# Stepping an encoder's background work twice per unit of weights

## The chip, the cores and the metric

One Trainium2 chip, one core. The metric is device microseconds of one execution, taken as the median of several; lower is better. The engines that matter here: TensorE (PE, matrix products), VectorE (DVE) and ScalarE (ACT) for elementwise work, GpSimd (POOL), and SyncE (SP), which issues the transfers. All of them work through their own queues in order, and meet at semaphores.

## The reference

Two layers of an encoder on 256 tokens of width 2048, all in float32. With `c` a condition vector, each layer computes

```
mod  = silu(c) @ ada_w + ada_b                # six vectors of 2048: scale, shift, gate, twice
h0   = rmsnorm(x) * (1 + scale0) + shift0
qA kA vA qB kB vB gateA gateB = split(h0 @ w_in)   # 8 heads of 128 in A (2 groups of k, v), 8 in B
a    = softmax(rotary, normed qA kA^T, |i-j| <= 128, sink per head) vA
b    = softmax(normed qB kB^T + 2-D relative bias, neighbourhood) vB
x   += gate0 * ((sigmoid(gateA) * (a @ w_proj_a) + sigmoid(gateB) * (b @ w_proj_b)) @ w_out)
h1   = rmsnorm(x) * (1 + scale1) + shift1
u    = depthwise conv over the tokens (width 3) of (h1 @ w_up);  g, v = halves of u, 5632 wide each
x   += gate1 * ((silu(g) * v) @ w_down)
```

## The kernel before, in words

**The stream.** All the weights of a layer lie in memory in the order in which they are used, cut into 232 units of 16 blocks of 128 x 128 floats (1 MB). `unit_steps` loads a unit (`w`, L337) and splits it into two float32r parts, in two halves of 8 blocks each: ScalarE casts the high part (`hl`, L348), VectorE subtracts it from the weights for the low part (L349). In the listings `hl_54_0` is the first half of unit 54. TensorE multiplies with both parts. `tokens` (L464 to 466) is used for q, k and v, three products 512 columns wide for each four blocks and each 128 tokens; `features` calls `feature_block` for everything else, either three products 256 wide per block (L395 to 397; the third takes the low part of the weights) or one of 512 and one of 256 (L391, L392). `Stream.at` counts the blocks of the current unit, `UB` is 16.

**The modulation.** The `mod` vectors are worked out on VectorE, 128 x 2048 products (`aw`, L248) in a fixed number by each unit (`plan`). They lie on the VectorE queue among the `hl` subtracts.

**The background.** The heads of the mixers, and the chunks of the normed `h`, are Python generators that emit a few instructions at each step. An object `bg` of the class `Paced` keeps the running ones with a rate and an accumulator. Whenever `features` or `tokens` have used up a unit (`at == UB`), they call `tick`: it first runs what was deferred to this point, then adds the rate to each accumulator and takes one step for each whole number in it. So the rate is steps per unit. It then lets `plan` emit modulation products.

The jobs are these. `attention` (L981 on) is one job for all 16 heads of a layer. One step of it gives each live head its next part, and starts one new head if its q and k are ready (`ready`, which for layer 0 has to be 3). The parts of a head, in `attend`: the scores `sc` (L727) and the softmax with them (DVE L730 with the mask and row maximum, `nm` L736; ACT exponentials L739, `es` L742; DVE `den` L743 and `ri` L745; ACT scaling of `p`, L747); then the transposes of `p` with the split of the result (`tp` L758, `pT`, ACT L481 and DVE L484); then the products with v (`po` L766) and their split (`oA`, L769 and L770). So one step holds `po` of head i, `tp` of head i+1, `sc` of head i+2 and the start of head i+3. In layer 1 the transposes are not TensorE's: VectorE transposes blocks of 32 x 32 (L326) and GpSimd copies them to their places (L320, 16 copies). Rates: `ATT` is 1.288 in layer 0 and 0.4 in layer 1; once the A heads are through (`attended`, ahead of the projection `proj_a`, which reads `oA` of all eight A heads, and which begins behind unit 52 in layer 0), layer 0 goes on with 0.36. The normed chunks of the next `h` have the rates `H_RATE`, 2.7 for the first and 1.7 for the second sub-layer. q and k are normed by instructions that `bg.defer` puts at unit ends (`qrs` L535 on GpSimd, `qn` L661 on VectorE, `packB` L698 on ScalarE).

**The order.** A list scheduler orders each engine's queue from the order in which the program emits the instructions and from its own costs. In layer 0 it may move the heads' instructions among those of the stream; in layer 1 they stay in the order of the program. So a step that is emitted half a unit sooner changes the queues of all engines around it.

## Time and profile before

| | |
|---|---|
| median of 3 runs | 2582.82 us (2582.07 to 2588.05) |
| the profiled execution | 2584.3 us |
| its span | 2581.7 us |
| mean granted clock of TensorE | 0.998 |
| TensorE busy | 2547.9 us, 99% |
| VectorE, ScalarE, GpSimd busy | 86%, 56%, 10% |
| waits of TensorE for `hl` of VectorE at L397, in all | 7.1 us in 9 |
| wait of TensorE for `p` at `tp` | 3.6 us in 4 |
| wait of TensorE for `packB` at `sc` | 2.6 us in 1 |

The span is the time between the first and the last instruction of the profiled execution. A row of the timeline gives the start and the length of an instruction (or of several alike in a row, xN), engine, line, operation, what is written and from what, and in brackets how long the engine had been idle before it and which instruction ended that. A row of the waits gives who waited for whom, the total, the number and the longest. Matrix products overlap, so their spacing is shorter than their length.

### The profile page before, as it was taken

The numbers are of one execution on the slowest core, as the hardware profiler recorded it, in microseconds if no ns is written. First come the engines' busy times: TensorE is split into PE (matmuls) and PEld (weight loads), VectorE is DVE, ScalarE is ACT, GpSimd is POOL, SyncE is SP. The second block draws the span as 40 slices with busy tenths as digits, with TensorE's granted clock in tenths as the row PEclk, the third lists the DMA queues.
The fourth block names the chain that finished last, engine by engine and source line by source line (L and its number), as shares of the span: only waits on it lengthen the run. The fifth ranks groups of instructions, "written<-read, shape, count | busy, mean of one in ns | idle before, by whom it ended". The sixth has DMA issues, their size and how long they took to land.

```text
span 2581.7 us, 43544 instructions
## 1 busy us (share of the span) xinstructions
PE 2547.9 (99%) x17324; PEld 2378.3 (92%) x17324; DVE 2212.6 (86%) x3227; ACT 1454.8 (56%) x2432; POOL 263.1 (10%) x345
## 2 busy tenths in 40 slices
PE   8999999999999999999999999999999999999999
PEld 7999899999999999999998879999999999999998
DVE  8998998998998899799987778879889987766775
ACT  5445765456663665466565566654576546644663
POOL 0001100000000000000003668730000000000000
PEclk9999999999999999999999999999999999999999
DMA  9998789986778778777767667778848775555554
GB/s 370 352 349 306 263 299 356 335 315 227 259 292 307 258 285 297 291 279 279 281 226 271 262 229 264 258 284 332 309 175 294 291 295 197 206 201 197 204 202 147
DMA packets 102158, 699.97 MB, mean 271 GB/s; under 512 B 12866, under 2 KB 15170, under 8 KB 18114
## 3 DMA queue, kind: packets, MB, share of 16 engines
q1 hardware_dynamic: 101954, 697.20, 73.0%
q8 instruction: 135, 2.21, 0.3%
q14 instruction: 69, 0.56, 0.1%
HBM read 695.06 MB, written 2.10 MB: 270 GB/s over the span
## 4 chain that ended last, share of the span: by engine, by line
PE 70%; DVE 14%; DMA 6%; ACT 4%; issue 4%; POOL 2%; SPq 0%; ACTq 0%; DVEq 0%; POOLq 0%
PE ps L391 31%; PE ps L392 15%; DVE hl L349 5%; PE ps L397 5%; PE ps L395 5%; PE ps L396 5%; DVE aw L248 4%; DMA aw<-in_aw 3%; PE ps_t L465 2%; PE ps_t L464 2%; PE ps_t L466 2%; ACT hl L348 2%; DMA w<-in_ws 2%; POOL p L320 1%; DVE x L1108 1%
## 5 line engine op out<-in xcount | busy, mean ns | idle before, releaser
L349 DVE TENSOR_TENSOR hl<-w,hl 128x1024 fp32r<-128x1024 f32 x928 | 1130.3, 1224 | 215.4 <-ACT hl L348 213.1
L348 ACT CAST hl<-w 128x1024 fp32r<-128x1024 f32 x928 | 964.7, 1046 | 587.0 <-PE ps L392 253.8
L391 PE MATMUL ps<-h,hl 128*128 128x512 f32 x2432 | 796.8, 382 | 0.0
L392 PE MATMUL ps<-h,hl 128*128 128x256 f32 x2432 | 662.9, 273 | 0.0
L391 PEld LDWEIGHTS ps<-h,hl 128*128 128x128 f32 x2432 | 459.7, 189 | 64.0
L392 PEld LDWEIGHTS ps<-h,hl 128*128 128x128 f32 x2432 | 466.9, 192 | 0.0
L248 DVE CUSTOM_DVE_ANT_0 aw<-aw,cact,ab 128x2048 f32<-128x2048 f32 x189 | 443.8, 2349 | 14.0 <-DMA aw<-in_aw 13.4
L395 PE MATMUL ps<-h,hl 128*128 128x256 f32 x896 | 247.3, 276 | 1.9 <-DVE ri L745 0.8
L397 PE MATMUL ps<-h,hl 128*128 128x256 f32 x896 | 245.9, 276 | 0.6 <-DVE hl L349 0.6
L396 PE MATMUL ps<-h,hl 128*128 128x256 f32 x896 | 246.4, 275 | 0.0
L465 PE MATMUL ps_t<-hl,h 128*128 128x512 f32 x576 | 220.4, 383 | 4.8 <-DVE hl L349 4.5
L464 PE MATMUL ps_t<-hl,h 128*128 128x512 f32 x576 | 217.7, 383 | 3.8 <-ACT h L571 2.4
L466 PE MATMUL ps_t<-hl,h 128*128 128x512 f32 x576 | 219.0, 381 | 0.0
L395 PEld LDWEIGHTS ps<-h,hl 128*128 128x128 f32 x896 | 171.9, 192 | 3.1 <-PE ps L397 0.9
L396 PEld LDWEIGHTS ps<-h,hl 128*128 128x128 f32 x896 | 172.0, 192 | 0.4 <-DVE h L572 0.2
L397 PEld LDWEIGHTS ps<-h,hl 128*128 128x128 f32 x896 | 171.6, 192 | 0.8 <-DVE hl L349 0.8
L391 PE MATMUL ps<-act_o,hl 128*128 128x512 f32 x512 | 170.5, 382 | 0.0
L1135 DVE SCALAR_TENSOR_TENSOR u<-both,cw,u 128x255 f32<-128x255 f32 x304 | 146.0, 480 | 3.8
L397 PE MATMUL ps<-merged,hl 128*128 128x256 f32 x512 | 140.8, 276 | 3.5 <-DVE hl L349 3.5
L395 PE MATMUL ps<-merged,hl 128*128 128x256 f32 x512 | 140.7, 275 | 0.4 <-ACT hl L348 0.4
L396 PE MATMUL ps<-merged,hl 128*128 128x256 f32 x512 | 140.6, 275 | 0.0
L392 PE MATMUL ps<-act_o,hl 128*128 128x256 f32 x512 | 139.6, 273 | 0.0
(242 smaller groups left out, 4867.6 us busy)
## 6 DMA issues: line engine op xcount, KB each, us to landing
w<-in_ws SPq DMA_DIRECT2D x463, 1024.0 KB, 4.9
aw<-in_aw SPq DMA_DIRECT2D x189, 1024.0 KB, 5.0
p<-in_bias SPq DMA_DIRECT2D x16, 256.0 KB, 4.9
x<-in_xT SPq DMA_DIRECT2D x4, 512.0 KB, 5.4
aw_o<-in_aw SPq DMA_DIRECT2D x2, 1024.0 KB, 12.8
out<-x SPq DMA_DIRECT2D x16, 128.0 KB, 2.2
w<-in_ws SPq DMA_DIRECT2D x2, 512.0 KB, 12.1
aw_b<-in_aw SPq DMA_DIRECT2D x1, 1024.0 KB, 17.9
```

The lines of the kernel that those rows point to most:

```text
L248: product = nc.vector.tensor_tensor_reduce(out=raw[:], in0=raw[:], in1=cact[:], scale=1.0, scalar=ab[:, i : i + 1], op0=ALU.mult, op1=ALU. ...
L348: nc.scalar.copy(hl[:, 0], r)
L349: nc.vector.tensor_tensor(out=hl[:, 1], in0=r, in1=hl[:, 0].bitcast(F32), op=ALU.subtract)
L391: nc.tensor.matmul(ps[:], hi, act.both, start=first, stop=False)
L392: nc.tensor.matmul(ps[:, :S], lo, act.high, start=False, stop=last)
L395: nc.tensor.matmul(out, hi, act[0], start=first, stop=False)
L396: nc.tensor.matmul(ps[:, :S], hi, act[1], start=False, stop=False)
L397: nc.tensor.matmul(out, lo, act[0], start=False, stop=last)
L464: nc.tensor.matmul(ps[:], xh, hi, start=kc == kcs[0], stop=False)
L465: nc.tensor.matmul(ps[:], xh, lo, start=False, stop=False)
L466: nc.tensor.matmul(ps[:], xl, hi, start=False, stop=kc == kcs[-1])
L1135: nc.vector.scalar_tensor_tensor(out=u[:, to], in0=ps[:, of], scalar=w[:, j : j + 1], in1=u[:, to], op0=ALU.mult, op1=ALU.add)
```

## The change

The accumulators gain half the rate at a time, and this is done twice per unit: `step` is what was the second half of `tick`, `tick` calls it at the unit's end as before, and a new `Stream.passed` calls it alone when half of the unit's blocks are used. The deferred instructions and the modulation's plan stay at unit ends. Rates are as they were.

```diff
             for fn in later:
                 fn()
+            self.step()
+
+        def step(self):
             for job in list(self.jobs):
-                job[2] += job[1]
+                job[2] += job[1] / 2
                 while job[2] >= 1.0:
...
+        def passed(self):
+            if self.at == UB:
+                self.tick()
+            elif self.at == UB // 2:
+                bg.step()
+
...
                     feature_block(ps, hl, j, act_of, i == 0, i == len(acts) - 1)
-                    if self.at == UB:
-                        self.tick()
+                    self.passed()
...
                     warm(WARM_ROW)
-                if self.at == UB:
-                    self.tick()
+                self.passed()
```

In the listings of the change line numbers are 3 higher from L291 on, and 7 higher behind L475 (`sc` L734, `tp` L765, `po` L773, `es` L749, `hl` L351 and L352).

What that does to the queues is shown at three places. The first is TensorE in layer 0 from the transposes of head 7 on (`tp`, with the scores of the next head, `sc`, put between them). Before:

```order
L758 MATMUL tp<-ident,p 128x128 x3
L727 MATMUL sc<-packB_0_224 128x256
L397 MATMUL ps_53_8_0_3375<-oA_4_2734,hl_52_1_3347 128x256
L395 MATMUL ps_53_8_0_3375<-oA_4_2734,hl_52_1_3347 128x256
L396 MATMUL ps_53_8_0_3375<-oA_4_2734,hl_52_1_3347 128x256
L766 MATMUL po<-pT,vA_1_2826 128x256 x2
L397 MATMUL ps_53_8_0_3375<-oA_4_2734,hl_52_1_3347 128x256
L395 MATMUL ps_53_8_0_3375<-oA_6_2848,hl_52_1_3347 128x256
L396 MATMUL ps_53_8_0_3375<-oA_6_2848,hl_52_1_3347 128x256
L397 MATMUL ps_53_8_0_3375<-oA_6_2848,hl_52_1_3347 128x256
L766 MATMUL po<-pT,vA_1_2826 128x256 x4
L395 MATMUL ps_53_16_0_3416<-oA_0_2446,hl_53_0_3419 128x256
```

With the change:

```order
L765 MATMUL tp<-ident,p 128x128 x3
L734 MATMUL sc<-packB_0_224 128x256
L773 MATMUL po<-pT,vA_1_2880 128x256 x6
L398 MATMUL ps_52_16_0_3303<-oA_7_3000,hl_52_0_3306 128x256
L398 MATMUL ps_53_8_0_3337<-oA_7_3000,hl_52_1_3309 128x256
L398 MATMUL ps_53_16_0_3378<-oA_7_3000,hl_53_0_3381 128x256
L398 MATMUL ps_54_8_0_3412<-oA_7_3000,hl_53_1_3384 128x256
L399 MATMUL ps_52_16_0_3303<-oA_7_3000,hl_52_0_3306 128x256
L400 MATMUL ps_52_16_0_3303<-oA_7_3000,hl_52_0_3306 128x256
L765 MATMUL tp<-ident,p 128x128
L734 MATMUL sc<-packB_0_224 128x256
L765 MATMUL tp<-ident,p 128x128 x3
```

The six products `po` and the first uses of `oA_7` now stand directly behind the transposes of head 7, and those of head 8 follow six products later, where a run of other products stood between them.

The second is VectorE at the same place, up to the low half of unit 54. Before:

```order
L770 TENSOR_TENSOR oA_7_2939<-po,oA_7_2939 128x256
L484 TENSOR_TENSOR vB_0_3209<-packB_0_224,vB_0_3209 128x256
L497 SCALAR_TENSOR_TENSOR ya_222<-ya_222,ps_52_16_0_3341 128x256
L745 RECIPROCAL ri<-den 128x2
L497 SCALAR_TENSOR_TENSOR ya_222<-ya_222,ps_53_8_0_3375 128x256
L497 SCALAR_TENSOR_TENSOR ya_222<-ya_222,ps_53_16_0_3416 128x256
L349 TENSOR_TENSOR hl_54_0_3516<-w_54_3514,hl_54_0_3516 128x1024
```

With the change (rows of the row maxima and repeats left out):

```order
L777 TENSOR_TENSOR oA_7_3000<-po,oA_7_3000 128x256
L491 TENSOR_TENSOR vB_0_3278<-packB_0_224,vB_0_3278 128x256
L248 ISA aw_46_3698,mod_172<-aw_46_3698,cact,ab_173 128x2048
L491 TENSOR_TENSOR pT<-tp,pT 128x512
L737 ISA p,m<-sc,p 128x256
L504 SCALAR_TENSOR_TENSOR ya_222<-ya_222,ps_52_16_0_3303 128x256
L743 TENSOR_SCALAR nm<-m 128x2
L504 SCALAR_TENSOR_TENSOR ya_222<-ya_222,ps_53_8_0_3337 128x256
L504 SCALAR_TENSOR_TENSOR ya_222<-ya_222,ps_53_16_0_3378 128x256
L504 SCALAR_TENSOR_TENSOR ya_222<-ya_222,ps_54_8_0_3412 128x256
L352 TENSOR_TENSOR hl_54_0_3479<-w_54_3477,hl_54_0_3479 128x1024
```

Between `oA_7` and the subtract for unit 54 there are now a modulation product, the `pT` of head 8, and the scores of the head behind it.

The third is ScalarE in layer 1, at the exponentials of head 1 (L739, then L746) and the cast of head 0's transposed weights (`pT`, L481, then L488). Before:

```order
L348 CAST hl_30_0_15157<-w_30_15155 128x1024
L348 CAST hl_30_1_15160<-w_30_15155 128x1024
L481 CAST qA_2_15118<-packA_14134 128x256
L481 CAST pT<-p 128x512
L739 ACTIVATE p,den<-p,nm 128x256 x2
L742 ACTIVATE es<-nm,sink_14275 128x2
L348 CAST hl_31_0_15239<-w_31_15237 128x1024
L348 CAST hl_31_1_15242<-w_31_15237 128x1024
L747 ACTIVATE p<-p,ri 128x256 x2
```

With the change:

```order
L351 CAST hl_30_0_15157<-w_30_15155 128x1024
L488 CAST qA_2_15106<-packA_14134 128x256
L746 ACTIVATE p,den<-p,nm 128x256 x2
L749 ACTIVATE es<-nm,sink_14275 128x2
L351 CAST hl_30_1_15160<-w_30_15155 128x1024
L754 ACTIVATE p<-p,ri 128x256 x2
L488 CAST pT<-p 128x512
L351 CAST hl_31_0_15239<-w_31_15237 128x1024
```

The exponentials and the scaling of head 1 now stand ahead of the cast `pT`, and one weight cast stands between them.

## The prediction

> **What bounds the kernel now.** I read the page's first part, then the waits of TensorE over the whole span, then the stretches in which those waits lie, then the instructions around the two largest.

> ```profile
> span 2581.7 us, 43544 instructions
> PE 2547.9 (99%) x17324; PEld 2378.3 (92%) x17324; DVE 2212.6 (86%) x3227; ACT 1454.8 (56%) x2432; POOL 263.1 (10%) x345
> ```

> TensorE is busy for 2547.9 of 2581.7 us. The change adds and removes no matrix product, so all it can win is in the remaining 34 us, and about half of that is the start. The waits of TensorE (total us, times, longest) say what is left:

> ```profile
> PE ps L397 <- DVE hl L349: 7.1, 9, 1.7
> PE ps_t L465 <- DVE hl L349: 4.5, 5, 2.8
> PE tp L758 <- ACT p L747: 3.6, 4, 2.4
> PE sc L727 <- ACT packB L698: 2.6, 1, 2.6
> PE ps L395 <- DVE ri L745: 0.8, 1, 0.8
> ```

> `tp` and `sc` are the transposes and the scores of the mixers' heads, so 3.6, 2.6 and 0.8 us belong to what the change re-times; of the 4.5 us before `ps_t`, 2.78 lie among the heads of layer 1 (below). The stretches of 50 us (PE, PEld, DVE, ACT and POOL busy, TensorE clock, DMA share, GB/s) show where the heads run:

> ```profile
> 250.00:300.00 50.00, 46.73 (x241) 40.25 (x240) 49.31 (x89) 37.52 (x106) 11.80 (x4) 1.00 0.79 286
> 300.00:350.00 50.00, 48.79 (x385) 45.65 (x385) 48.03 (x107) 40.95 (x107) 2.45 (x1) 1.00 0.66 236
> 350.00:400.00 50.00, 49.90 (x427) 48.82 (x426) 48.04 (x80) 30.02 (x58) 0.00 (x0) 1.00 0.92 340
> 1450.00:1500.00 50.00, 47.70 (x235) 41.26 (x233) 36.05 (x56) 32.89 (x69) 31.98 (x49) 1.00 0.61 232
> 1500.00:1550.00 50.00, 46.43 (x224) 40.69 (x225) 41.65 (x69) 31.89 (x73) 29.02 (x47) 0.93 0.63 232
> 1550.00:1600.00 50.00, 50.00 (x410) 48.82 (x409) 42.75 (x68) 32.76 (x69) 43.82 (x61) 1.00 0.73 262
> ```

> In layer 0 (250 to 350) VectorE is full: 49.31 and 48.03 of 50. TensorE lacks 3.27 and 1.21 us, and one unit of weights needs two `hl` subtracts of VectorE, so there the order of VectorE's work decides. In layer 1 (1450 to 1550) VectorE has 8 to 14 us to spare per stretch, TensorE lacks 2.30 and 3.57, the clock drops to 0.93, and GpSimd is in the chain. Two places then, one of each kind.

> **The change, first place: the eight A heads of layer 0.** Before, the accumulator gains 1.288 at each unit's end and so takes two steps in units 44, 47 and 51. Now it gains 0.644 twice. The start of head 0 needs `ready` to be 3, which comes in unit 44; the half step at unit 44's middle is spent on nothing, and the half steps from then on give one turn less before the stream reaches `proj_a`: head 7's products `po` come at the end of unit 52 instead of 51. By the orders, 24 matmuls of 512 columns more precede the first scores (235 matmuls, nearly all so wide, fill 47.70 us in 1450 to 1500, 0.20 each: 4.9 us). The stretch between the first scores and the first transposes holds the same TensorE work (7.1 us counted in both orders), so the largest wait there, 2.37 us at 274.70, I leave as it is; a chain of the same instructions stands before it.

> ```profile
> 274.70 0.33 PE L758 MATMUL tp<-ident,p 128*128 128x128 f32 x1 [2.37 <-ACT p L747]
> ...
> 333.67 0.91 ACT L747 ACTIVATE p<-p,ri 128x256 f32<-128x256 f32 x2 [0.83 <-DVE ri L745]
> ...
> 335.98 0.69 DVE L484 TENSOR_TENSOR pT<-tp,pT 128x512 fp32r<-128x512 f32 x1
> 336.59 0.41 DVE L730 CUSTOM_DVE_ANT_0 p<-sc,p 128x256 f32<-128x256 f32 x1
> ...
> 337.27 2.35 DVE L248 CUSTOM_DVE_ANT_0 aw<-aw,cact,ab 128x2048 f32<-128x2048 f32 x1
> ...
> 339.55 0.17 DVE L736 TENSOR_SCALAR nm<-m 128x2 f32<-128x2 f32 x1
> 339.62 0.42 DVE L770 TENSOR_TENSOR oA<-po,oA 128x256 fp32r<-128x256 f32 x1
> ...
> 340.25 0.49 ACT L739 ACTIVATE p<-p,nm 128x256 f32<-128x256 f32 x1
> ...
> 341.30 0.73 DVE L497 SCALAR_TENSOR_TENSOR ya<-ya,ps 128x256 f32<-128x256 f32 x2
> 341.96 1.23 DVE L349 TENSOR_TENSOR hl<-w,hl 128x1024 fp32r<-128x1024 f32 x1
> ...
> 345.54 0.28 PE L397 MATMUL ps<-oA,hl 128*128 128x256 f32 x1
> ```

> What is late next is the low half of unit 54, `hl_54_0`. Now its VectorE queue: counted from `hl_44_0`, the instructions ahead of it grow by two `aw` products (2 x 2.3, 337.27 to 339.55), one `pT` (0.6), one pair of `L730` for a B head (2 x 0.34, 336.59 and the like), an `L497` (0.33) and small ones: 4.6 + 0.6 + 0.7 + 0.3 = 6.2 us. TensorE's work ahead of its first use of that half grows by only 1.6 us (matmuls of both orders counted, 0.12 each for 256 columns by the 427 in 49.90 us of 350 to 400). Before, the half was ready at 341.96 + 1.23 = 343.2 and first read at 345.54: a slack of 2.35. So 6.2 - 1.6 - 2.35 = **+2.2 us** of new wait, spread over `tp` of heads 7 and 8, `oA_7` and `hl_54_0`. Later VectorE work is two products lighter, but TensorE cannot make up time. Bounds: if the products run in waits that VectorE had anyway, at most one counts: 2.3 less, -0.1, taken with other shifts as -1. If the turns pay their own chains instead with little beside them, +4.6 (worked out at the first rival), rounded to +5. I take +2.2, since VectorE's idle time in these 100 us is only 0.69 + 1.97.

> The B heads of layer 0, paced at 0.36, slip by up to 2.5 units. Their work is under 48.04 of 50 busy VectorE at first and TensorE loses 0.10 in 350 to 400; `proj_b` reads them long after. Cost 0; if that cover were gone, one half step is half a unit, 2.5 us by the 4.9 above.

> **Second place: heads 1 to 3 of layer 1.** The rate 0.4 gave steps 2 and 3 units apart at unit ends (units 19, 21, 24, 26, 29, 31, 34); now they are 2.5 units apart, so every other step comes half a unit, 2.5 us, earlier and the others stay. Here the transposes go through VectorE (L326) and GpSimd copies (L320), one head after the other:

> ```profile
> 1457.86 13.90 POOL L320 COPY p<-spare 32x128 f32<-32x128 f32 x16 [7.87 <-DVE spare L326]
> 1471.80 0.62 ACT L481 CAST pT<-p 128x512 fp32r<-128x512 f32 x1 [5.68 <-POOL p L320]
> 1473.63 0.16 DVE L743 TENSOR_TENSOR den<-den,es 128x2 f32<-128x2 f32 x1 [2.67 <-ACT es L742]
> 1474.56 2.36 DVE L349 TENSOR_TENSOR hl<-w,hl 128x1024 fp32r<-128x1024 f32 x2
> 1476.84 0.70 DVE L326 STREAM_TRANSPOSE packA<-p 128x512 f32<-128x512 f32 x1
> 1477.61 8.34 POOL L320 COPY p<-packA 32x128 f32<-32x128 f32 x16 [5.84 <-DVE packA L326]
> 1485.98 0.71 DVE L326 STREAM_TRANSPOSE packA<-p 128x512 f32<-128x512 f32 x1 [2.49 <-POOL p L320]
> 1486.75 9.97 POOL L320 COPY p<-packA 32x128 f32<-32x128 f32 x16 [0.81 <-DVE packA L326]
> 1496.81 1.64 POOL L535 TENSOR_TENSOR qrs<-qss,mhalf 128x8 f32<-128x8 f32 x1
> 1498.48 1.29 DVE L661 TENSOR_TENSOR qn<-ps_t,qrs 128x512 f32<-128x512 f32 x2 [5.85 <-POOL qrs L535]
> 1499.68 2.35 DVE L349 TENSOR_TENSOR hl<-w,hl 128x1024 fp32r<-128x1024 f32 x2
> 1500.95 0.48 PE L465 MATMUL ps_t<-hl,h 128*128 128x512 f32 x1 [2.78 <-DVE hl L349]
> 1507.91 0.16 DVE L745 RECIPROCAL ri<-den 128x2 f32<-128x2 f32 x1
> 1511.51 1.27 ACT L698 ACTIVATE packB<-qtp,gains 128x512 f32<-128x512 f32 x2
> 1512.25 1.65 PE L727 MATMUL sc<-kA,qA 128*128 128x256 f32 x6 [2.62 <-ACT packB L698]
> ```

> ScalarE's `pT` stands before head 1's exponentials, waits 5.68 us for head 0's copies, and VectorE's `den` waits 2.67 behind it; only after two more `hl` subtracts comes L326, the copies of heads 1 and 2 follow end to end, and `qn` waits 5.85 for the `qrs` queued on GpSimd behind them. That wait holds `hl_35_0`, and TensorE stands 2.78 us. In the new order the scores of head 1 come half a unit earlier and the exponentials stand ahead of `pT`, and L326 of head 1 comes two `hl` subtracts earlier, straight behind VectorE's `pT`. Then: copies of head 0 end at 1471.8 as before, ScalarE `pT` to 1472.4, VectorE `pT` 0.6, L326 at 1473.0 (was 1476.84, -3.8); head 1's copies end 8.4 + 0.8 later at 1482.2 if they cost the same beside other VectorE work; L326 of head 2 at 1482.3 (was 1485.98); its copies and `qrs` (9.97 + 1.64 and the gaps) end at 1494.8 instead of 1498.45. So `qn` is 3.6 us earlier, `hl_35_0` ends at 1494.8 + 1.2 + 1.2 = 1497.2, and TensorE asks for it at 1500.95 - 2.78 = 1498.2: that wait is gone. But the scores at 1512.25 wait for the accumulator that `packB` leaves, behind a chain from `qn` (L661 1498.48, `ri` 1507.91, L747, two casts, `packB` 1511.51). The chain moves up by 3.6 at most; what TensorE lost to its clock before it (0.07 of 50 us are 3.5 us around two waits, some 1.7 each) lies inside that wait and pays nothing by itself. I take **-3.3 us**, the shift less a little for the reordered `oA`. Bounds: 0, if another instruction in that chain is the last; -5.4 if both waits (2.78 + 2.62) go.

> The three rows of copies differ: 16 of them took 13.90, 8.34 and 9.97 us with other VectorE work beside them. [...]

> **The normed chunks of h.** Rates 1.7 and 2.7 gave one to three chunks at a unit's end; now they come one or two at a time and up to half a unit sooner. Their VectorE and ScalarE work is the same and lies beside the products of two to eight units; no wait of TensorE on them is among the rows above. I take 0; a half unit of bunching undone or made is 2.5 us at most, and I put ±0.5 on it.

> Sum: +2.2 - 3.3 + 0 = -1.1. The profiled execution took 2584.3 us (span 2581.7 and 2.6 around it), 1.5 above the median of 2582.8, so I apply the sum to the median: **2581.7 us**.

> **The rivals.**

> First, slower: the turns of heads 7 and 8 collide. Between their two `tp`, the old order has 5.6 us of other matmuls, the new one 0.7 and `po` of head 7 (0.7), and up to the next `tp` 2.6 and another `po`. A turn's chain, two L730 (0.8), `pT` (0.6), `nm` (0.1), two exponentials (1.0), `ri` (0.1), L747 (0.9), is 3.5 us, and an `aw` in it adds 2.3. From the point at which TensorE has less than that beside it, the two turns pay: 3.5 - 1.4 = 2.1 and 5.8 - 3.3 = 2.5. With the wait for `hl_54_0` in full (2.2) and a half clock behind the longest (1.7) that is +8.5, with nothing won in layer 1: 2591.3 us. For it: VectorE full. Against it: the 2.37 at 274.70 lies in a stretch whose clock is 1.00.

> [...]

> Second, faster: even steps clear both places, 2.37 + 1.2 in layer 0, 2.78 + 2.62 and 1.7 of half clock in layer 1: -10.7, 2572.1 us. Against it: the sum of VectorE's work above.

> Third, nothing won in layer 1: the copies fall beside other `aw` and `hl`, or the wait at 1500.95 moves to 1512.25. Then +2.2 stands alone: 2585.0 us. That the steps don't move is excluded by the orders; that they move without effect in both places is 2582.8, and belongs here.

> **How the numbers follow.** Forecast 0.47 (its own range 2578 to 2585), slower 0.16, faster 0.12, nothing won 0.25. A measurement of this kernel can tell 0.3%, 7.7 us, from no change: below 2575.1 or above 2590.6. The forecast and the third rival lie inside; of the first rival about three quarters lie outside, of the second nearly all: faster 0.11, same 0.77, slower 0.12. The range runs from 2574 to 2591, which cuts off most of the second rival and a part of the first.

> **What would show it.** Right: the wait of TensorE on `hl` near 1500 gone or under 1 us, the one on `packB` still there and some 3 us earlier, L326 of head 1 near 1473, `tp`, `oA_7` and `hl_54_0` waits between 335 and 352 summing to some 2 us or more, where there was none over 0.1, and 250 to 300 as before. Wrong: a wait on `qrs` or `p` of 5 us or more at a new place, copies of 13 us for head 1, a clock under 1.00 in 300 to 350, or new waits in units 57 to 73 or where the normed chunks lie.

## The result, and the profile after

The change made the kernel slower: 2596.94 us median of 6 runs (2594.09 to 2598.45) against 2583.28 us, a ratio of 1.0036 with a 95% interval of 1.0026 to 1.0046, +9.3 us (6.7 to 11.9). The forecast was 2581.7 us with a range from 2574 to 2591. The ratio on record is less than the quotient of these two medians, which lie 13.7 us apart; in the later experiments the kernel before had medians of 2587.3 to 2588.0 us, and 2596.94 is 9 to 10 above those. Here and below a difference is the ratio turned into microseconds with 2583.

The first part of the page, after:

```profile
span 2592.9 us, 43535 instructions
...
PE 2552.2 (98%) x17324; PEld 2380.7 (92%) x17324; DVE 2213.8 (85%) x3227; ACT 1455.8 (56%) x2432; POOL 251.3 (10%) x345
```

The same count of instructions on each engine and 11.2 us more span: the rest of this section looks for the waits and for a slower clock (PE's 4.3 us more of busy time are mostly matmuls at such a clock: up to the last matmul the granted clock is at half, 0.50, for 6.8 us before and for 13.7 after, and half of the difference is some 3.4, an estimate). The waits of TensorE after (total us, times, longest):

```profile
PE ps L400 <- DVE hl L352: 7.7, 9, 2.0
PE tp L765 <- ACT p L754: 6.0, 4, 2.9
PE ps_t L473 <- DVE hl L352: 3.8, 6, 1.2
PE sc L734 <- ACT packB L705: 3.3, 1, 3.3
...
PE ps L398 <- ACT oA L776: 1.2, 1, 1.2
PE ps L398 <- DVE m L504: 1.1, 1, 1.1
PE ps L398 <- DVE ya L1061: 0.9, 2, 0.7
```

`tp` went from 3.6 to 6.0 us, and the last three groups shown are new: `oA`, `m` (the merged branches that the last projection of the sub-layer reads) and `ya`. The 2.8 us for `hl` among the `ps_t`, forecast to go, shrank to 1.23 and 0.76. The stretches, after (columns as above):

```profile
250.00:300.00 50.00, 47.11 (x235) 40.72 (x234) 48.83 (x82) 36.29 (x99) 11.37 (x4) 0.97 0.75 273
300.00:350.00 50.00, 45.44 (x343) 41.32 (x342) 44.84 (x99) 36.40 (x100) 1.64 (x1) 0.98 0.64 241
350.00:400.00 50.00, 48.66 (x415) 47.69 (x414) 46.66 (x82) 29.43 (x53) 0.00 (x0) 0.99 0.83 310
...
500.00:550.00 50.00, 48.85 (x438) 48.66 (x437) 47.05 (x85) 24.49 (x45) 0.00 (x0) 1.00 0.79 291
...
1450.00:1500.00 50.00, 49.62 (x248) 43.62 (x248) 40.22 (x58) 33.08 (x71) 37.41 (x46) 1.00 0.69 261
1500.00:1550.00 50.00, 44.73 (x211) 38.47 (x211) 35.63 (x59) 30.86 (x68) 26.99 (x54) 0.93 0.59 226
```

Between 300 and 350 TensorE ran 343 matrix instructions instead of 385, and VectorE, full before (48.03), was idle for 5.16 us instead of 1.97.

To say where time went, I summed over each trace by how much the distance between the starts of neighbouring matmuls exceeds the median for their line and shape (shorter distances count against it); this counts waits and slow clock alike. In us:

| kernel | heads of layer 0 (250 to 450) | 450 to 700 | heads of layer 1 (1400 to 1600) | 1700 to 2000 | whole run |
|---|---|---|---|---|---|
| before | 15.2 | 4.2 | 10.9 | 10.0 | 56.6 |
| the change | 22.8 | 6.0 | 10.3 | 12.3 | 67.2 |
| layer 0's attention in halves | 21.5 | 10.7 | 11.4 | 9.7 | 69.0 |
| layer 1's attention in halves | 14.9 | 3.2 | 7.4 | 7.6 | 48.1 |
| the change, head 0 scored as before | 15.8 | 7.2 | 10.1 | 12.6 | 61.3 |
| both attentions in halves, head 0 scored as before | 16.6 | 6.0 | 10.3 | 11.2 | 59.9 |

(The last four are experiments below.) So 7.6 of the 10.6 us are lost at the heads of layer 0, 7.0 of them between 340 and 360 (2.4 before, 9.4 after); layer 1's heads gave 0.6.

Each row is one execution, and the other columns can't be put down to the change. The change and layer 0's attention alone have the same queues on all engines up to unit 102 of layer 0, near 620 us, and lose 6.0 and 10.7 between 450 and 700. The second and the last of the experiments have the same queues from the end of layer 0's heads on, and lose 7.6 and 11.2 between 1700 and 2000. The sums of the whole run follow the spans to some 3 us (layer 1's attention alone: 8.5 less by the sums, 5.5 by the span). At the heads of layer 0 executions with the same queues agree better: 22.8 and 21.5 in the first pair, and 15.2 and 14.9 in the kernel before and the one with half steps in layer 1 alone.

TensorE's waits at heads 7 and 8, and VectorE beside them (with one row of ScalarE), after:

```profile
342.23 0.33 PE L765 MATMUL tp<-ident,p 128*128 128x128 f32 x1 [1.50 <-ACT p L754]
...
343.99 0.49 PE L773 MATMUL po<-pT,vA 128*128 128x256 f32 x2 [0.24 <-ACT pT L488]
344.88 0.71 PE L773 MATMUL po<-pT,vA 128*128 128x256 f32 x4 [0.40 <-DVE pT L491]
346.80 0.71 PE L398 MATMUL ps<-oA,hl 128*128 128x256 f32 x4 [1.21 <-ACT oA L776]
```

```profile
337.78 0.17 DVE L743 TENSOR_SCALAR nm<-m 128x2 f32<-128x2 f32 x1
338.32 0.42 DVE L777 TENSOR_TENSOR oA<-po,oA 128x256 fp32r<-128x256 f32 x1 [0.37 <-ACT oA L776]
338.94 2.35 DVE L248 CUSTOM_DVE_ANT_0 aw<-aw,cact,ab 128x2048 f32<-128x2048 f32 x1 [0.20 <-DMA aw<-in_aw]
339.18 0.28 ACT L749 ACTIVATE es<-nm,sink 128x2 f32<-128x2 f32 x1
...
341.22 0.15 DVE L750 TENSOR_TENSOR den<-den,es 128x2 f32<-128x2 f32 x1
...
343.79 0.42 DVE L737 CUSTOM_DVE_ANT_0 p<-sc,p 128x256 f32<-128x256 f32 x1 [2.22 <-PE sc L734]
...
352.60 1.22 DVE L352 TENSOR_TENSOR hl<-w,hl 128x1024 fp32r<-128x1024 f32 x1
```

The same head before:

```profile
330.68 0.16 DVE L736 TENSOR_SCALAR nm<-m 128x2 f32<-128x2 f32 x1
330.75 2.34 DVE L248 CUSTOM_DVE_ANT_0 aw<-aw,cact,ab 128x2048 f32<-128x2048 f32 x1
333.02 0.15 DVE L743 TENSOR_TENSOR den<-den,es 128x2 f32<-128x2 f32 x1
334.23 0.33 PE L758 MATMUL tp<-ident,p 128*128 128x128 f32 x1
```

Read the second fence from the top: a modulation product stands between `nm` and `den` of head 7's softmax. The exponentials (`es` is the last of them) were done at 339.46, so it holds `den` for 1.8 us. Such a product stood there before too, but TensorE then had other matrix products until `tp` and did not wait. Now it has nothing left but that head and waits 1.50 at `tp`; the scores that come with this `tp` are what VectorE needs next, so VectorE waits 2.22 for TensorE; and the low half of unit 54, at 341.96 before, starts at 352.60. The two engines wait for each other in turn.

### The profile page after: what moved, and what is told of

It reads as the page before. It is cut to its first block, busy times and chain, and to the rows that moved or that the text cites. A ratio compares the mean times of both kernels' runs of the same rounds, so it can differ in the third digit from the quotient of the medians.

```text
span 2592.9 us, 43535 instructions
## 1 busy us (share of the span) xinstructions
PE 2552.2 (98%) x17324; PEld 2380.7 (92%) x17324; DVE 2213.8 (85%) x3227; ACT 1455.8 (56%) x2432; POOL 251.3 (10%) x345
## 5 line engine op out<-in xcount | busy, mean ns | idle before, releaser
L352 DVE TENSOR_TENSOR hl<-w,hl 128x1024 fp32r<-128x1024 f32 x928 | 1130.9, 1225 | 226.5 <-ACT hl L351 224.3
L351 ACT CAST hl<-w 128x1024 fp32r<-128x1024 f32 x928 | 965.3, 1046 | 580.2 <-PE ps L395 254.1
L395 PE MATMUL ps<-h,hl 128*128 128x256 f32 x2432 | 663.1, 273 | 0.5 <-DVE hl L352 0.5
L395 PEld LDWEIGHTS ps<-h,hl 128*128 128x128 f32 x2432 | 466.9, 192 | 1.1 <-DVE hl L352 1.1
L248 DVE CUSTOM_DVE_ANT_0 aw<-aw,cact,ab 128x2048 f32<-128x2048 f32 x189 | 444.2, 2351 | 19.0 <-DMA aw<-in_aw 18.6
L395 PE MATMUL ps<-act_o,hl 128*128 128x256 f32 x512 | 139.6, 273 | 0.0
```

The costliest lines, as they stand in the source:

```text
L248: product = nc.vector.tensor_tensor_reduce(out=raw[:], in0=raw[:], in1=cact[:], scale=1.0, scalar=ab[:, i : i + 1], op0=ALU.mult, op1=ALU. ...
L351: nc.scalar.copy(hl[:, 0], r)
L352: nc.vector.tensor_tensor(out=hl[:, 1], in0=r, in1=hl[:, 0].bitcast(F32), op=ALU.subtract)
L395: nc.tensor.matmul(ps[:, :S], lo, act.high, start=False, stop=last)
```

## The experiments

"+" is slower than the kernel before.

**Which part of the change.** The accumulators get a flag, so that a job may step in halves or at unit ends:

```diff
-            self.jobs.append([gen, rate, late])
+            self.jobs.append([gen, rate, late, halves])
...
+                if not (job[3] or end):
+                    continue
-                job[2] += job[1] / 2
+                job[2] += job[1] / 2 if job[3] else job[1]
```

*Layer 0's attention alone:*

> Half steps for the attention of layer 0 alone; everything else steps at unit ends. Theory L (the turn that layer 0's A heads lose before proj_a is the loss): most of the 9 to 13 us of the change is here, +8 to +11 against before, with layer 0's waits as with the change (tp of head 8 near 342, oA_7, tp 9) and the clock under 1.00 behind them. Rival S (the loss is spread over the later places, units 87 and 98 to 112): +4 or less.

Measured: ratio 1.0033 (1.0020 to 1.0045), +8.5 us. (The `tp` near 342 that is called head 8's here, and in one expectation below, is head 7's in the rest of the text, where the first head is head 0.) *Layer 1's attention alone:*

> Half steps for the attention of layer 1 alone. Theory L: -1 to +1 against before: the wait on packB at sc comes 1.9 us earlier as it does with the change, and part of that is given back at half clock. Rival S: +2 to +4, as the merged products of layer 1 (units 98 to 112) wait longer.

Measured: 0.9986 (0.9977 to 0.9996), -3.6 us, better than any theory had it here, and near the prediction's own term for this place (-3.3). *The chunks of normed `h` alone:*

> Half steps for the chunks of normed h alone; both attentions step at unit ends. If spreading the chunks is free, as forecast: -0.5 to +0.5 us against before. Rival N (bunching the chunks at unit ends cost VectorE's queue something): -2 or better. With the change 2.0 us were lost behind unit 98 of layer 1; if the chunks cause it, +2 here.

Measured: 1.0009 (1.0000 to 1.0018), +2.3 us with an interval that begins at 0. It is at the edge of what can be told, and not a gain. Its trace loses 1.6 us more than before between 450 and 700, but 1.1 of them ahead of 620, where its queues are still those of the kernel before, so that is not the edit's. The three sum to +7.2, within the interval of the change. *The A heads of layer 0 alone, its B heads back at unit ends:*

```diff
             bg.pace(job, 0.36)
+            bg.whole(job)
```

> Half steps for the eight A heads of layer 0 alone; its B heads go back to unit ends at rate 0.36 (one unit later than before the change, as the A heads end a unit later). If the A heads are the loss: +6 to +9 against before, like the half steps for the whole of layer 0's attention (+8.5). If the B heads' half positions count: +4 or less.

Measured: 1.0023 (1.0012 to 1.0034), +5.9 us. So the A heads are most of layer 0's loss. That the B heads are the other 2.6 is not shown, as the intervals overlap.

**The lost turn or the half positions?** First the turn is lost without any half step, with whole steps and a lower rate:

```diff
-ATT = [1.288, 0.4]
+ATT = [1.20, 0.4]
```

> The kernel before, all steps at unit ends, with layer 0's rate lowered from 1.288 to 1.20: head 0 starts at the end of unit 44, head 7's products come at the end of unit 52, one turn later, as with the change. Theory L: +6 to +11 with no half step anywhere. Rival H: within 3 us of before.

Measured: 1.0013 (1.0002 to 1.0023), +3.4 us: less than theory L, more than nothing. Then half steps with a higher rate, so that head 7's step comes where it came before the change:

```diff
-ATT = [1.288, 0.4]
+ATT = [1.40, 0.4]
```

> Half steps for the attention of layer 0 alone, with its rate raised from 1.288 to 1.40, so that head 0 still starts at the end of unit 44 and head 7's products come at the end of unit 51, as before the change. Theory L: the loss goes, -1 to +2 against before. Rival H (the half positions themselves are bad, since a turn in the middle of a unit meets the casts of the other half): it stays at +6 or more.

Measured: 1.0048 (1.0034 to 1.0061), +12.4 us. This seemed to speak for rival H, and theory L in its first form fell: to end the steps sooner gains nothing. TensorE's order of this kernel showed why. Its `po` of head 7 stood where it stands with the change (1968 matrix products ahead of it in both, 1922 before), although its step is emitted a unit sooner; and head 0's scores, which start the chain, stood 12 products later than before (24 with the change). In the kernel before, unit 44 has two steps: the first starts head 0, the second computes its scores. With half steps, and also with whole ones at 1.20, the scores come a step later. That gave a third theory, C: the A heads run as fast as VectorE lets them, and it is the start of the chain that was moved. Its test keeps all half steps of the change, and only lets the step that starts head 0 go on to the next one:

```diff
                     todo.pop(0)
+                    if l == 0 and len(todo) == HA + HB - 1:
+                        continue
                 yield
```

> The change, with one edit: in layer 0 the step that starts head 0 goes straight on to the next one, so that head 0's scores come at the end of unit 44, as they did before the change (there unit 44 had two steps). All steps are still halves. VectorE's work ahead of the low half of unit 54 is then what it was before. Theory C (the A heads of layer 0 run as fast as VectorE lets them, whatever the steps; the turn lost at the start is what arrives late at proj_a): the loss of layer 0's A heads goes, in all -4 to +1 against before, as layer 1 keeps its gain. Rival H (half positions are bad in layer 0): +5 or more.

Measured: 0.9997 (0.9988 to 1.0005), -0.8 us. The loss of 9.3 us is gone with half steps everywhere, so half positions are not bad by themselves, and rival H falls in that form. The stretches of this kernel:

```profile
250.00:300.00 50.00, 47.35 (x241) 40.02 (x240) 48.94 (x88) 38.60 (x106) 10.68 (x4) 1.00 0.74 274
300.00:350.00 50.00, 48.13 (x381) 45.05 (x380) 48.23 (x107) 39.81 (x105) 1.64 (x1) 1.00 0.67 246
```

VectorE is full again (48.23) and TensorE runs 381 instructions in the second stretch, 385 before. By the table above the heads of layer 0 lose 15.8 us, 15.2 before.

This run moves the start of the chain and, with it, its end. And a late chain alone is not the whole price: with whole steps at 1.20 the first scores and head 7's `po` stand as late in TensorE's queue as with the change, for +3.4 only. What goes with the price is VectorE's queue between `hl_44_0` and `hl_54_0`. This is what it has more than in the kernel before, an estimate: the instructions counted in the queues, with the times that the prediction read from the rows:

| kernel | VectorE's work more, us | measured, us |
|---|---|---|
| the change, head 0 scored as before; both attentions in halves, the same (below) | 0 | -0.8; -2.1 |
| whole steps at 1.20 (one modulation product, one `L497`) | 2.6 | +3.4 |
| the change; layer 0's attention alone; its A heads alone | 6.2 | +9.3; +8.5; +5.9 |
| half steps at 1.40 (the 6.2, and one `oB` and one `vB`) | 6.9 | +12.4 |

The order of the prices is that of the work. But the intervals of neighbours overlap, and the kernels differ in what layer 1 and the chunks add, so this supports theory C and does not prove it.

**Why a late chain costs that much.** If VectorE's queue is the reason, lighter work there must make the loss small. Fourteen modulation products beside the A heads, made 128 x 64 in both kernels:

```diff
-                    out=raw[:], in0=raw[:], in1=cact[:], scale=1.0, ...
+                    out=raw[:, :w_], in0=raw[:, :w_], in1=cact[:, :w_], scale=1.0, ...
```

> The change, with 14 modulation products of layer 0 (numbers 36 to 49, those that run beside the A heads) cut from 128 x 2048 to 128 x 64, so that VectorE has some 30 us less to do between units 42 and 60; the modulation is no longer the reference's. Theory V (VectorE's queue: a product of 2.3 us stands between nm and den of a head, and there is no slack to take the lost turn): against the kernel before with the same cut the change then costs -4 to +2. Rival P (TensorE's four open accumulators wait for oA_7, whatever VectorE has to do): the change still costs +6 or more.

> The kernel before with the same cut of the 14 products, as the base of the run above. Theory V: faster than before by some 3 us, the waits of the A heads in layer 0 (4.5 us). Rival P: within 1.5 us of before.

Measured: the change with the cut 1.0003 (0.9994 to 1.0013), the kernel before with the cut 1.0028 (1.0017 to 1.0040). So the change costs -6.5 us there (theory V had -4 to +2), and the waits at heads 7 and 8 are not there at all:

```profile
300.00:350.00 50.00, 49.70 (x386) 46.06 (x384) 41.23 (x112) 43.05 (x113) 1.64 (x1) 1.00 0.75 278
```

But the base missed what was expected of it: with 30 us less to do on VectorE it is 7 us slower. The list scheduler, which knows of the cut, orders layer 0 anew, and by the trace this base waits 1.59 us near 415, 0.94 near 495 and 2.83 in two near 528. The cut is too large an edit to price the change with. So a smaller one: only products 44 to 46, the ones among the last A heads, with the same edit and another range.

> The change, with three modulation products of layer 0 (numbers 44 to 46, those among the last A heads) cut from 128 x 2048 to 128 x 64; TensorE's order around heads 7 and 8 stays, VectorE has 6.9 us less to do there, and the modulation is no longer the reference's. Theory V (these products stand in the chains of heads 7 and 8): the waits at tp 8, po and oA_7 (3.4 us) and the late hl_54_0 go, and the run is 4 to 7 us faster than the change, +2 to +5 against before. Rival P (four accumulators are open and wait for oA_7 anyway): +7 or more.

> The kernel before with the same three products cut, as the base of the run above. Theory V: within 1.5 us of before, since TensorE hardly waited there.

Measured: 1.0009 (1.0000 to 1.0017) with the change, +2.3 us, and 0.9994 (0.9984 to 1.0004) for the base, both as theory V had them. The cut is worth 7.0 us to the change (9.3 - 2.3) and 1.5 to the kernel before, whose interval includes no change at all. The three products take 0.28 us each instead of 2.35, 6.2 us of work in all, so with the change about all of it was on the path. But the orders did not stay as expected: three and six other products now stand ahead of and among the `po` of head 7, and `hl_54_0` comes ahead of head 8's `pT` on VectorE, so a part of the 7.0 may be the new order's. `tp` of head 7 then waits 0.03 us and `po` not at all; `oA_7` still waits:

```profile
345.29 0.71 PE L399 MATMUL ps<-oA,hl 128*128 128x256 f32 x4 [0.87 <-ACT oA L777]
```

So VectorE's queue, work and order together, accounts for most of the collision, and in this order some 0.9 us of it stay with the four open accumulators (rival P).

**Both attentions in halves, with the start put back.** Half steps for both attentions, head 0 started and scored as before, chunks at unit ends:

> Half steps for both attentions, head 0 of layer 0 started and scored at the end of unit 44 as in the run with the moved start, and the chunks of normed h at unit ends. Theory C: -5 to -1 against before, faster than both kernels. Rival H: +3 or more.

Measured: 0.9992 (0.9982 to 1.0002), -2.1 us, not told apart from before. The kernel with half steps in layer 1's attention alone has the lowest ratio of all that ran, 0.9986, and the only interval that lies below 1.

## Why the prediction was wrong

**The part on layer 1 held in its mechanism.** L326 of head 1 was forecast near 1473, was 1476.84. With the change (9.3 us later in the trace by then) and GpSimd's copies:

```profile
1482.53 0.71 DVE L329 STREAM_TRANSPOSE packA<-p 128x512 f32<-128x512 f32 x1
```

```profile
1467.20 14.04 POOL L323 COPY p<-spare 32x128 f32<-32x128 f32 x16 [7.88 <-DVE spare L329]
1483.36 9.93 POOL L323 COPY p<-packA 32x128 f32<-32x128 f32 x16 [2.12 <-ACT hl L351]
1494.10 10.00 POOL L323 COPY p<-packA 32x128 f32<-32x128 f32 x16 [0.81 <-DVE packA L329]
1504.18 1.64 POOL L542 TENSOR_TENSOR qrs<-qss,mhalf 128x8 f32<-128x8 f32 x1
```

1482.53 - 9.3 = 1473.2. But head 1's copies took 9.93 us, not the 8.34 that I carried over from before, so `qn` was 1.9 us earlier (1505.85 - 9.3 = 1496.6, was 1498.48) and not 3.6: the size of that step was wrong, by what the third rival had named. Of head 1's sixteen copies five took 1.14 to 1.26 us, each beside an `hl` subtract (before, three took 1.20 to 1.37, beside such a subtract too); those with no VectorE instruction beside them took 0.28 to 0.30 in both. The wait of 2.78 shrank to 1.23 and 0.76, and the one on `packB` came 1.9 us sooner, as a chain that moves up. Alone this edit measured -3.6 us, of which the 1.9 explain about half, so that it comes so close to -3.3 is luck. In its profile, the fastest of its 12 runs, the heads of layer 1 lose 3.5 us less than before (10.9 to 7.4). The other 1.6 are half clock behind the wait on `packB`, which I had put inside that wait: before, the clock was at half from 1512.01 to 1515.43, and in this profile at no time there. With the change twice as much half clock followed the same wait (6.83 us, from 1518.60 to 1525.42, against 3.41), which is why the heads of layer 1 gave only 0.6 there (last section).

**The part on layer 0 failed, in its sum for `hl_54_0`.** I added VectorE's new instructions ahead of it (6.2), took off TensorE's new work and the old slack, and got +2.2. The new instructions were counted rightly. What failed is the sentence "since VectorE's idle time in these 100 us is only 0.69 + 1.97": it took VectorE to stay full. With the change VectorE was idle for 5.16 us between 300 and 350, since the scores it had to work on came from a TensorE that was itself waiting for VectorE. So `hl_54_0` started 10.6 us later rather than 6.2. In place of +2.2, TensorE stood 4.7 us between 340 and 360 (1.50, 0.24, 0.40 and 1.21 above, and 1.33 at a later `tp`, at 356.70) and ran 3.4 us at half clock (0.50 from 347.82 to 351.24), 1.7 us lost, a term that the sum did not have; by the sums of the table 7.0 us more than before were lost there. Measured alone, layer 0's attention cost 8.5. The first rival had this mechanism and its place, at a chance of 0.16; I had set the forecast above it by an argument on totals, where the question was one of order. Its price, +8.5, is right in the two turns (4.6) and the half clock (1.7) and lucky in the rest: with the change TensorE did not wait for `hl_54_0` at all (the rival had 2.2). Its other half, nothing won in layer 1, did not hold for the edit alone.

**"The largest wait there, 2.37 us at 274.70, I leave as it is" failed too.** It became

```profile
280.08 0.47 PE L765 MATMUL tp<-ident,p 128*128 128x128 f32 x1 [2.89 <-ACT p L754]
```

half a microsecond longer, and behind it the clock fell (0.97 in its stretch, where it had been 1.00). The same wait stands in the runs in which the chain starts late (2.86 with whole steps at 1.20, 3.64 with half steps at 1.40), and is 2.38 again in the run with the start put back. The fall of the clock is not settled by the half microsecond: 2.87 with the A heads alone in halves did not bring it, and 2.37 in the run with the chunks alone did.

**The lost turn was named, but as a matter of where the turns end.** The prediction wrote "the half steps from then on give one turn less before the stream reaches `proj_a`". The run at rate 1.40, with the turns' end put back and no gain, shows that the end alone was not the point; the run with the start put back, whose end moves with it, points to the scores of head 0.

**The terms taken as 0 stay open.** "Cost 0" for the B heads of layer 0: the sums have 1.8 us more lost between 450 and 700 with the change, among them a wait of 1.15 us for `m` at 530.57 where TensorE had none before. But two executions with the same queues differ by 4.7 there, and a wait for `m` of 1.21 stands at 527.64 with the chunks alone in halves, where the queues are still those of the kernel before. It is there also with three products cut from the kernel before (1.20). So neither move of the change is needed for it, and why it comes and goes is not known. "I take 0" for the chunks: +2.3 (0 to 4.6), not told apart from nothing.

## What to carry to other kernels

Where two engines feed each other and one is full, an edit that makes work arrive later cannot be priced by adding that work up and taking off slack (here that gave +2.2 us, and 7.0 were lost there): look in the order for the place at which both have nothing left but each other's result, and count each chain in full there. Before a small loss is put down to an edit, see whether the queues differ where it lies: two kernels with the same queues differed by 4.7 us in one stretch here. When an accumulator's grain is changed, look first at its first steps: rounding moves the start of a chain, and a chain that something else limits does not make that up (here head 0's scores stood 24 products later in TensorE's queue, and head 7's `po` still 46). And try a pacing change job by job; here one of three jobs gained 3.6 us and another lost 8.5.

## What the hardware showed that was not expected

In these traces the length of a wait of TensorE does not by itself decide whether its clock drops. In layer 1, at the same instruction (`sc` behind `packB`), a wait of 3.27 us with the change was followed by half clock (granted 0.50 from 1518.60 to 1525.42), and one of 3.28 with layer 1's attention alone in halves was not (1.00 from 1500 to 1550):

```profile
1519.63 1.65 PE L734 MATMUL sc<-kA,qA 128*128 128x256 f32 x6 [3.27 <-ACT packB L705]
...
1521.92 0.63 PE L472 MATMUL ps_t<-hl,h 128*128 128x512 f32 x1
1522.35 0.63 PE L473 MATMUL ps_t<-hl,h 128*128 128x512 f32 x1
```

```profile
1509.78 0.94 PE L736 MATMUL sc<-kA,qA 128*128 128x256 f32 x6 [3.28 <-ACT packB L707]
...
1510.56 0.38 PE L475 MATMUL ps_t<-hl,h 128*128 128x512 f32 x1
1510.77 0.38 PE L476 MATMUL ps_t<-hl,h 128*128 128x512 f32 x1
```

Neighbours start 0.43 us apart in the first and 0.21 in the second, for some ten of them: over 2 us for the same wait. In the run with the chunks alone in halves, 2.77 us before `ps_t` brought the drop and 2.88 before `sc` did not; with layer 0's attention alone it was 2.81 that did not.

So waits of 3.27 and 3.28 us differed here by over 2 us in what they cost, and by these counts the difference is where they came to lie: an edit that only shifts a wait can gain or lose that much. A single profile's clock is no property of the kernel: the six runs of the change had mean clocks of 0.997 to 0.999.
